# A further combined k-pair in seven paired products of a hybrid decoder layer

## The chip, the cores and the metric

The kernel runs on one core of a Trainium2 chip. The metric is the time of one execution on the device, in microseconds (us). The time before is the median of 3 runs, 1982.21 us (1981.88 to 1982.49). A profile of one further execution gives the times of single instructions. Engines are named as in the profile: PE is TensorE (matmuls), PEld its loading of the stationary operand, DVE is VectorE, ACT is ScalarE, POOL is GpSimd, SP is SyncE, which issues the DMAs.

## The reference

One decoder layer in float32 over 256 tokens of width 2048:

```python
hn = rmsnorm(h, norm_mix_w)
q, k, v, g_ret, xr, yr, g_a, g_b = jnp.split(hn @ w_in, offsets, axis=-1)
ret_out = silu(g_ret) * head_groupnorm(chunkwise_retention(q, k, v), ret_gn_w)
rnn_out = gelu(yr) * rg_lru(causal_dwconv(xr))
merged = sigmoid(g_a) * (ret_out @ w_proj_ret) + sigmoid(g_b) * (rnn_out @ w_proj_rnn)
h = h + merged @ w_mix_out
h = h + memory_cross_attention(rmsnorm(h, norm_xa_w), rmsnorm(mem), w_q, w_k, w_v, w_o)
gate, val = jnp.split(causal_dwconv(rmsnorm(h, norm_ffn_w) @ w_up), 2, axis=-1)
h = h + (silu(gate) * val) @ w_down
out = rmsnorm(h, final_norm_w)
```

Nearly all of the work is in the products with weights: `w_in` is 2048 x 14336, the projections are 2048 x 2048, `w_up` is 2048 x 11264 and `w_down` 5632 x 2048. The feed-forward width of 5632 is done in three parts of 4, 4 and 3 blocks of 512 columns.

## The kernel before

**Split operands.** Every operand of a product is held as two numbers of the type fp32r, `hi` (the value rounded) and `lo` (what the rounding left). A product of two tiles is then three matmuls: hi x hi, lo x hi, hi x lo (`products_n`, `rows_of`). For weights, ScalarE writes `hi` as a cast (L349) and VectorE writes `lo` as a difference (L350), for two slices of 128 rows at a time (128 x 1024). There are 6 buffers for `hi` and 6 for `lo` (`PART_BUFS`), and 3 for raw weights (`RAW_BUFS`), which SP loads in one order fixed on the host (`weight_stream`).

**Products.** `steps_n` computes 256 tokens x 512 columns. It walks over the inner dimension in chunks of four slices. `steps_pair` computes two such blocks of 512 columns at once and walks in k-pairs, two slices of 128 rows at a time: eight k-pairs for an inner dimension of 2048. A plain k-pair is 8 tile products, 24 matmuls. They go into four banks of PSUM: `p2` and `p4` for the first block of columns (two token halves), `x3` and `n` for the second.

**Combined k-pairs.** For the k-pairs listed in the tuple `seven`, the pair is treated as a 2 x 2 block product (token halves by slices, slices by column blocks) and computed with seven products in place of eight, by sums of blocks in the manner of Strassen and Winograd: 21 matmuls. This needs

- four sums of weight blocks on VectorE, in place in the raw buffer (L370 in `seven_parts`), and seven weight parts to split in place of four: three splits of 128 x 1024 and one of 128 x 512;
- sums of the token blocks, made once per operand and kept (`sums_of`, L448 to L459): one sum of hi and lo where the unsplit value is gone, three differences `tq`, a cast by ScalarE and a difference `ts`;
- four more banks of PSUM, `p1`, `p6`, `p7`, `x5`. After the last k-pair in the tuple, a copy by ScalarE (L513) and four operations of VectorE (L520) bring them together as `o`, and after the last k-pair of the product four more (L530) add `p2`, `p4`, `x3` and `n`.

The tuples are `SEVEN = (2, 5)` for most pairs, `SEVEN_O = (3, 5)` for the attention's output, `SEVEN_U = (4,)` for the up products, and `SEVEN_V = (5,)` for the second pair of values.

**Order of the work.** `weight_plan` lists the products: q, k, v and gates of the retention in two groups; eight products of the recurrent branch with their conversions between; the gate `g_b` and `w_proj_rnn`, alternating; two pairs for `g_a` (columns from O_GA, "first" and "second gate pair") and two for `w_proj_ret`; `w_mix_out`; attention; then the feed-forward parts. In these, one up pair (a gate block and its value block) precedes the down products of the part before, and the others follow: up 0 to 3, up 4, down of part one, up 5 to 7, up 8, down of part two, up 9 and 10, last down. A down product of the first two parts is two pairs, each with the four blocks' hidden activations `hid` (eight k-pairs) as its left operand.

Inside a product, `chunks` prefetches weights two chunks ahead and, after each chunk, runs what `later(n, ...)` has put off by n chunks: turning finished rows by DMA (`by_dma`, two copies to `pl` by ScalarE, a DMA transpose, two copies back as `f`, L565), splitting the heads of the retention (`split_head`, during the two `g_a` pairs), the convolutions of the up products (L1136, L1138) and their gates (`gate_up`, L1147 to L1150, with splits at L588 and L589). Matmuls keep the order in which they are written. On the other engines a scheduler of the compiler decides the order in the queue, with a priority for some steps; once built, every queue is fixed and works in order, so that a late instruction delays all that stand behind it.

Of the kernel before, what the change touches and what calls it, by code (L numbers as in the profile page):

```python
# [38 lines left out]
GN_EPS = 1e-5  # L39
FF_PARTS = [4, 4, 3]  # L40
EARLY = [2, 2, 4, 4, 4]
SEVEN = (2, 5)
SEVEN_O = (3, 5)
SEVEN_U = (4,)
SEVEN_V = (5,)

O_Q, O_K, O_V, O_G = 0, 1024, 2048, 4096
O_XR, O_YR, O_GA, O_GB = 6144, 8192, 10240, 12288
# [26 lines left out]
def weight_plan():  # L75

    plan = []
    for g in range(2):
        keys = [("w_in", 0, NT, c + g * BW) for c in (O_Q, O_K)]
        values = [("w_in", 0, NT, O_V + b * BW) for b in range(2)]  # L80
        plan += keys + [both("w_in", O_V + 1024, SEVEN_V)] if g else [keys[0], values[0], keys[1], values[1]]
        plan.append(both("w_in", O_G + g * 1024))
    for b in range(4):
        plan += [("w_in", 0, NT, c + b * BW) for c in (O_XR, O_YR)]
    plan += [("w_in", 0, NT, O_GB + b * BW) for b in range(2)] + [both("w_proj_rnn", 0)]
    plan += [both("w_in", O_GB + 1024), both("w_proj_rnn", 1024)]
    plan += [both(w, c + b * BW) for w, c in (("w_in", O_GA), ("w_proj_ret", 0)) for b in (0, 2)]
    plan += [("w_mix_out", 0, NT, b * BW) for b in range(4)]
    plan += [(w, 0, NT, b * BW) for b in range(4) for w in ("xa_w_k", "xa_w_q")]
    plan += [("xa_w_v", 0, NT, b * BW) for b in range(4)]  # L90
    plan += [both("xa_w_o", 0, SEVEN_O)] + [("xa_w_o", 0, NT, b * BW) for b in (2, 3)]
    for kind, *a in ff_plan():
        if kind == "down" and sum(a) < NF // 4:
            plan += [both("ffn_w_down", b * BW, SEVEN, a[0] * BW, 4 * a[1]) for b in (0, 2)]
        elif kind == "down":
            plan += [("ffn_w_down", a[0] * BW, 4 * a[1], b * BW) for b in range(4)]
        else:
            plan.append(both("ffn_w_up", a[0] * BW, SEVEN_U, apart=FF))
    return plan


# [64 lines left out]
def hybrid_layer(  # L166
# [305 lines left out]
            sums_of(t, src, scale)  # L472
        out.append(t)

    def steps_pair(w, row, st, nk, c1, c2, seven=SEVEN):

        last = max(seven)
        banks, begun = {}, set()
        banks["p2"], banks["p4"] = (lambda a: (a[:, 0, :], a[:, 1, :]))(acc())
        banks["x3"], banks["n"] = (small((P, BW)) for _ in range(2))  # L480

        def rows_of(name, left, right, end):

            o = banks[name]
            for i, (a, b) in enumerate(((0, 0), (1, 0), (0, 1))):
                mm(o, left[a], right[b], start=name not in begun, stop=end and i == 2, skip_group_check=True)
                begun.add(name)

        o1 = o2 = None
        for k0, n, parts in chunks(nk, w, row, (c1, c2, seven)):  # L490
            k2 = k0 // KH
            for i in seven:
                if k2 < i <= k2 + 3 and (not isinstance(st, list) or i < len(st)):
                    sums_of(st[i])
            t = st[k2]
            own = [
                [(t[:, j, i * P : (i + 1) * P], t[:, j, S + i * P : S + (i + 1) * P]) for j in range(2)]
                for i in range(2)
            ]
            if k2 in seven:  # L500
                if "p1" not in banks:
                    for a, b in (("p1", "p6"), ("p7", "x5")):
                        two = acc()
                        banks[a], banks[b] = two[:, 0, :], two[:, 1, :]
                ts = sums_of(t)
                s3, s1, s2, s4 = ((ts[:, 0, i, :], ts[:, 1, i, :]) for i in range(4))
                lefts = (own[0][0], s4, own[0][1], s1, s3, s2, own[1][1])
                for name, l, r in zip(("p1", "x3", "p2", "x5", "p7", "p6", "p4"), lefts, parts):
                    rows_of(name, l, r, k2 == last and name in ("p1", "x5", "p7", "p6"))
                if k2 == last:  # L510
                    o1, o2 = (big([P, 2, BW], s="o") for _ in range(2))
                    with tc.high_priority(FREE):
                        act.copy(o1[:, 0, :], banks["p1"])  # L513
                        for o, a, b, op in (
                            (o2[:, 0, :], o1[:, 0, :], banks["p6"], ALU.add),
                            (o1[:, 1, :], o2[:, 0, :], banks["p7"], ALU.add),
                            (o2[:, 1, :], banks["x5"], o1[:, 1, :], ALU.subtract),
                            (o2[:, 0, :], banks["x5"], o2[:, 0, :], ALU.subtract),
                        ):
                            dve.tensor_tensor(out=o, in0=a, in1=b, op=op)  # L520
            else:
                end = k0 + n == nk
                for b, names in enumerate((("p2", "p4"), ("x3", "n"))):
                    for tt, name in enumerate(names):
                        for j in range(KH):
                            rows_of(name, own[tt][j], parts[b * KH + j], end and j == KH - 1)
            yield o1, o2
        with tc.high_priority(FREE):
            for o, a in ((o1[:, 0, :], "p2"), (o1[:, 1, :], "p4"), (o2[:, 0, :], "x3"), (o2[:, 1, :], "n")):
                dve.tensor_tensor(out=o, in0=o, in1=banks[a], op=ALU.add)  # L530
# [212 lines left out]
    def split_head(h):  # L743
        f = words[h // 2][:, 2 * (h % 2) : 2 * (h % 2) + 2, :]
        ret.append(split_cols(f, lambda j: half_gn[:, 2 * h + j : 2 * h + j + 1]))
        if h in SEVEN:
            sums_of(ret[h])

    def retain(g, qr, kr, vs, dec, gates):
# [63 lines left out]
    for g in range(2):  # L813
        dec = big([P, 4, S], s="dec")
        vs, turned = [], ([], [])
        for b, o in enumerate((O_Q, O_K)):

            def rotate_both(f, o=turned[b]):
                o.append(rotated(f[:, 0:2, :]))
                later(0, lambda: o.append(rotated(f[:, 2:4, :])))  # L820

            a = gemm_n("w_in", 0, xs, NT, o + g * BW) if g + b else q0
            turned_rows(a, rs0, rotate_both, 2 - b if g + b else 3, g + b > 0)
            if b == 1:
                sp.dma_start(
                    out=dec,
                    in_=consts[:, C_DEC + g * 4 * S : C_DEC + (g + 1) * 4 * S].rearrange("p (h s) -> p h s", s=S),
                )
            if g == 0:
                v = gemm_n("w_in", 0, xs, NT, O_V + b * BW) if b else ended(v_steps)  # L830
                vs.append(split_rows(v, rs0))
        if g == 1:
            vs += [split_rows(v, rs0) for v in pair("w_in", 0, xs, NT, O_V + 1024, O_V + 1024 + BW, SEVEN_V)]
        qr, kr = turned
        gates = []
        c = O_G + g * 1024
        for a in pair("w_in", 0, xs, NT, c, c + BW):
            t = big([P, 2, BW], s="gate")
            for tt in range(2):
                act.activation(t[:, tt, :], a[:, tt, :], AF.Tanh, scale=half_rs0[:, tt : tt + 1])  # L840
            dve.scalar_tensor_tensor(out=a, in0=t, scalar=1.0, in1=a, op0=ALU.add, op1=ALU.mult)
            gates.append(a)
        retain(g, qr, kr, vs, dec, gates)
# [164 lines left out]
    def residual(w, st, out, wcol, steps=None):  # L1008
# [4 lines left out]
        for b in range(4):  # L1013
            if steps:
                steps(b)
                if b == 0:
                    for one in products[:3]:
                        for _ in range(2):
                            next(one)
            elif b == 0:  # L1020
                sources += pair(w, 0, st, NT, 0, BW, SEVEN_O)
            h = hrow[b]
            dve.tensor_add(h, h, sources.pop(0) if sources else ended(products[b]))
            by_dma(h, lambda f, b=b: turn(f, b, out, wcol), 1 + (b == 1), b == 3 and steps is None)
            if b < 2:
                later(2 + b, lambda h=h, b=b: squares(h, ss, b))
            else:
                squares(h, ss, b)
# [211 lines left out]
    def up(b, hid, seven):  # L1240
# [4 lines left out]
            conv(f, NF + 4 * b, vl)  # L1245
            gate_up(gt, vl, hid, seven)

        two = pair("ffn_w_up", 0, h2s, NT, b * BW, FF + b * BW, SEVEN_U)
        for a, then, wait in zip(two, (lambda f: conv(f, 4 * b, gt), value), (1, 3)):
            with tc.high_priority(FREE):  # L1250
                for tt in range(2):
# [4 lines left out]
    for kind, b, *n in ff_plan():  # L1256
        if kind == "up":
            b0 = max(one[1] for one in ff_plan() if one[0] == "down" and one[1] <= b)
            seven = tuple(i - 2 * (b - b0) for i in SEVEN) if b0 < sum(FF_PARTS[:2]) else ()
            up(b, hid.setdefault(b, []), seven)  # L1260
        else:
            final = b + n[0] == NF // 4
# [48 lines left out]
```

## Time and profile before

| what | value |
|---|---|
| median of 3 runs | 1982.21 us |
| profiled execution | 1980.76 us |
| its span, from the first to the last instruction | 1979.0 us |
| PE busy | 1965.8 us, 99% |
| DVE busy | 1564.5 us, 79% |
| ACT busy | 1367.1 us, 69% |
| granted TensorE clock, mean | 0.999 |

A row of a group of instructions reads: line, engine, operation, output<-inputs, shapes, x count | busy us, mean ns of one | idle time of the engine ahead of them, and what ended it. A row of the timeline reads: start, length, engine, line, operation, output<-inputs, x count of instructions merged, and in brackets the engine's idle time ahead of it with what ended it. A row of waits reads: engine, line <- what it waited for: us in total, times, longest. Successive instructions of an engine overlap a little, so that busy time is less than count times mean.

### The profile page before, as it was taken

To read this page: it belongs to the slowest core of one execution; us is meant where nothing else is said; L and a number is where in the kernel's file an instruction comes from. 1 tells how busy PE (TensorE), PEld (TensorE's weight loads), DVE (VectorE), ACT (ScalarE), POOL (GpSimd) and SP (SyncE) were. 2 spreads that over 40 slices of the span, in tenths; PEclk is the share of its full clock that TensorE was granted. 3 is DMA by queue.
4 is the path that set the end of the run, shared out by engine and by line. 5 is a ranking of instruction groups with operands and counts; after the bars stand their busy time and mean duration, and the time that the engine had idled before them with its cause. 6 is when DMAs were issued, how large, how long until landed. Compare 5 with 4: busy or idle time off the path is not lost.

```text
span 1979.0 us, 24013 instructions
## 1 busy us (share of the span) xinstructions
PE 1965.8 (99%) x8834; PEld 1631.4 (82%) x8834; DVE 1564.5 (79%) x2050; ACT 1367.1 (69%) x1671; POOL 26.8 (1%) x25
## 2 busy tenths in 40 slices
PE   9999999999999999999999999999999999999998
PEld 7888788888888888888888888888888888888887
DVE  6887986899898888767555567778889878898686
ACT  7666657989654656697676667777776578774683
POOL 0000010010000000000000000000000000000000
PEclk9999999999999999999999999999999999999999
DMA  9755567666555465887676657666666566666673
GB/s 334 238 213 173 194 232 203 213 210 212 194 212 189 176 228 192 297 277 226 218 222 206 203 170 223 210 216 213 224 207 208 212 211 215 215 210 233 214 252 110
DMA packets 197190, 425.62 MB, mean 215 GB/s; under 512 B 142032, under 2 KB 146640, under 8 KB 152016
## 3 DMA queue, kind: packets, MB, share of 16 engines
q1 hardware_dynamic: 197072, 424.09, 64.2%
q8 instruction: 69, 1.13, 0.2%
q14 instruction: 49, 0.40, 0.1%
HBM read 388.39 MB, written 2.10 MB: 197 GB/s over the span
## 4 chain that ended last, share of the span: by engine, by line
PE 91%; DVE 3%; ACT 3%; issue 1%; DMA 1%; SPq 0%; POOL 0%; POOLq 0%; DVEq 0%; ACTq 0%
PE acc L251 66%; PE sm L251 25%; DVE lo L350 1%; DMA raw<-in_wall 1%; ACT hi L349 1%; ACT f L565 1%; ACT pl L552 0%; DMA pt<-pl 0%; DVE xr L932 0%; DVE tb L734 0%; ACT rows L804 0%; DMA raw<-in_head 0%; DVE fv L1138 0%; DVE o L530 0%; DVE raw L370 0%
## 5 line engine op out<-in xcount | busy, mean ns | idle before, releaser
L251 PE MATMUL acc<-hi,s 128*128 128x512 f32 (+1 forms) x3976 | 1218.7, 388 | 0.2 <-ACT s L611 0.2
L350 DVE TENSOR_TENSOR lo<-raw,hi 128x1024 fp32r<-128x1024 f32 (+1 forms) x794 | 931.8, 1197 | 325.7 <-ACT hi L349 315.8
L349 ACT CAST hi<-raw 128x1024 fp32r<-128x1024 f32 (+1 forms) x794 | 788.3, 1023 | 401.1 <-PE acc L251 126.6
L251 PEld LDWEIGHTS acc<-hi,s 128*128 128x128 f32 x3976 | 743.4, 188 | 152.4 <-ACT s L611 0.5
L251 PE MATMUL acc<-lo,s 128*128 128x512 f32 (+1 forms) x1988 | 771.0, 388 | 1.4 <-DVE lo L350 1.4
L251 PEld LDWEIGHTS acc<-lo,s 128*128 128x128 f32 x1988 | 373.3, 188 | 79.8 <-DVE lo L350 3.1
L251 PE MATMUL sm<-hi,s 128*128 128x512 f32 x1344 | 414.0, 389 | 1.6 <-DVE o L530 1.6
L251 PEld LDWEIGHTS sm<-hi,s 128*128 128x128 f32 x1344 | 252.1, 188 | 55.0 <-ACT v L600 1.8
L251 PE MATMUL sm<-lo,s 128*128 128x512 f32 x672 | 261.5, 389 | 0.0
L565 ACT COPY f<-pt 128x1024 uint16<-128x1024 uint16 x128 | 167.1, 1353 | 36.2 <-DMA pt<-pl 35.8
L251 PEld LDWEIGHTS sm<-lo,s 128*128 128x128 f32 x672 | 126.2, 188 | 26.1
L370 DVE TENSOR_TENSOR raw<-raw 128x512 f32<-128x512 f32 x160 | 110.0, 687 | 2.4
L251 PE MATMUL acc<-hi,ts 128*128 128x512 f32 x240 | 73.9, 389 | 0.0
L552 ACT COPY pl<-rows 128x1024 uint16<-128x1024 uint16 x56 | 55.7, 1042 | 24.8 <-DVE rows L576 13.3
L552 ACT COPY pl<-o 128x1024 uint16<-128x1024 uint16 x52 | 51.6, 1038 | 6.7 <-DVE o L1000 6.7
L251 PEld LDWEIGHTS acc<-hi,ts 128*128 128x128 f32 x240 | 45.0, 188 | 9.3
L251 PE MATMUL acc<-lo,ts 128*128 128x512 f32 x120 | 47.1, 393 | 1.4 <-DVE lo L350 1.3
L1138 DVE SCALAR_TENSOR_TENSOR fv<-f,pf,fv 128x255 f32<-128x255 f32 (+1 forms) x88 | 38.3, 476 | 0.0
L530 DVE TENSOR_TENSOR o<-o,acc 128x512 f32<-128x512 f32 x52 | 33.2, 678 | 5.7 <-PE acc L251 5.7
L1138 DVE SCALAR_TENSOR_TENSOR fg<-f,pf,fg 128x255 f32<-128x255 f32 (+1 forms) x88 | 35.8, 477 | 0.0
L520 DVE TENSOR_TENSOR o<-o,acc 128x512 f32<-128x512 f32 x52 | 35.2, 678 | 0.0
L530 DVE TENSOR_TENSOR o<-o,sm 128x512 f32<-128x512 f32 x52 | 33.9, 677 | 0.1
(190 smaller groups left out, 1010.8 us busy)
## 6 DMA issues: line engine op xcount, KB each, us to landing
raw<-in_wall SPq DMA_DIRECT2D x352, 1024.0 KB, 4.9
nat<-in_x SPq DMA_DIRECT2D x8, 512.0 KB, 9.2
raw<-in_wall SPq DMA_DIRECT2D x7, 512.0 KB, 6.2
pt<-pl SPq DMA_TRANSPOSE x128, 3.3
nat<-in_mem SPq DMA_DIRECT2D x4, 512.0 KB, 8.9
xt<-in_x_t SPq DMA_DIRECT2D x3, 512.0 KB, 9.3
xt<-in_mem_t SPq DMA_DIRECT2D x3, 512.0 KB, 6.4
dec<-in_consts SPq DMA_DIRECT2D x2, 512.0 KB, 4.4
```

The source lines that it names most:

```text
L251: tc.keep_in_program_order(pe.matmul(*a, **k))
L349: act.copy(hi[:, cs], src[:, cs])
L350: dve.tensor_tensor(out=lo[:, cs], in0=src[:, cs], in1=hi[:, cs].bitcast(F32), op=ALU.subtract)
L370: dve.tensor_tensor(out=o, in0=a, in1=b, op=ALU.add)
L520: dve.tensor_tensor(out=o, in0=a, in1=b, op=op)
L530: dve.tensor_tensor(out=o, in0=o, in1=banks[a], op=ALU.add)
L552: act.copy(planes[:, tt], words[:, tt])
L565: act.copy(halves_[:, :, :, cs], turned_[:, :, :, cs])
L1138: dve.scalar_tensor_tensor(out=y[:, s:S], in0=z[:, j, 0 : S - s], scalar=pf[:, 2 - s, t : t + 1], in1=y[:, s:S], op0=ALU.mult, op1=ALU.add,)
```

## The change

- `SEVEN` becomes (2, 6) in place of (2, 5), and `SEVEN_V` becomes (6,) in place of (5,): in these pairs the last combined k-pair is k-pair 6.
- A new tuple `MORE = (2, 4, 6)` is used for the second gate pair, the second pair of `w_proj_ret`, and the second pair of both paired down products: three combined k-pairs in place of two.
- A new tuple `MORE_U = (2, 4)` is used for the up pair that follows something other than an up pair in the plan (blocks 0, 5 and 9): two in place of one.
- Token sums are made for heads 2, 4 and 6 of `ret` and for the matching tiles of `hid`, in place of 2 and 5.
- `steps_pair` reads its tuple from the plan, and is not given it any more.

Nothing else is edited. The host packs the weights of a combined k-pair in another order of slices, as before.

```diff
-SEVEN = (2, 5)
+SEVEN = (2, 6)
+MORE = (2, 4, 6)
 SEVEN_O = (3, 5)
 SEVEN_U = (4,)
-SEVEN_V = (5,)
+MORE_U = (2, 4)
+SEVEN_V = (6,)
...
-    plan += [both(w, c + b * BW) for w, c in (("w_in", O_GA), ("w_proj_ret", 0)) for b in (0, 2)]
+    for w, c in (("w_in", O_GA), ("w_proj_ret", 0)):
+        plan += [both(w, c), both(w, c + 1024, MORE)]
...
-            plan += [both("ffn_w_down", b * BW, SEVEN, a[0] * BW, 4 * a[1]) for b in (0, 2)]
+            plan += [both("ffn_w_down", b * BW, MORE if b else SEVEN, a[0] * BW, 4 * a[1]) for b in (0, 2)]
...
-            plan.append(both("ffn_w_up", a[0] * BW, SEVEN_U, apart=FF))
+            plan.append(both("ffn_w_up", a[0] * BW, MORE_U if plan[-1][0] != "ffn_w_up" else SEVEN_U, apart=FF))
...
-    def steps_pair(w, row, st, nk, c1, c2, seven=SEVEN):
+    def steps_pair(w, row, st, nk, c1, c2):
+        seven = plan[gemms[0]][3][2]
...
-        if h in SEVEN:
+        if h in MORE:
             sums_of(ret[h])
...
-            seven = tuple(i - 2 * (b - b0) for i in SEVEN) if b0 < sum(FF_PARTS[:2]) else ()
+            seven = tuple(i - 2 * (b - b0) for i in MORE) if b0 < sum(FF_PARTS[:2]) else ()
```

More of the change, by code (lines that the diff above doesn't have):

```diff
@@ L832, in hybrid_layer @@
         if g == 1:
-            vs += [split_rows(v, rs0) for v in pair("w_in", 0, xs, NT, O_V + 1024, O_V + 1024 + BW, SEVEN_V)]
+            vs += [split_rows(v, rs0) for v in pair("w_in", 0, xs, NT, O_V + 1024, O_V + 1024 + BW)]
         qr, kr = turned
@@ L1020, in residual @@
             elif b == 0:
-                sources += pair(w, 0, st, NT, 0, BW, SEVEN_O)
+                sources += pair(w, 0, st, NT, 0, BW)
             h = hrow[b]
@@ L1246, in value @@
             gate_up(gt, vl, hid, seven)
-        two = pair("ffn_w_up", 0, h2s, NT, b * BW, FF + b * BW, SEVEN_U)
+        two = pair("ffn_w_up", 0, h2s, NT, b * BW, FF + b * BW)
         for a, then, wait in zip(two, (lambda f: conv(f, 4 * b, gt), value), (1, 3)):
```

## The prediction

> **What bounds the kernel now.** I read the busy shares first, then the chain that ended last, then who waits for whom on TensorE, and last busy time by stage.
>
> ```profile
> span 1979.0 us, 24013 instructions
> PE 1965.8 (99%) x8834; PEld 1631.4 (82%) x8834; DVE 1564.5 (79%) x2050; ACT 1367.1 (69%) x1671; POOL 26.8 (1%) x25
> PE 91%; DVE 3%; ACT 3%; issue 1%; DMA 1%; SPq 0%; POOL 0%; POOLq 0%; DVEq 0%; ACTq 0%
> 1219.43 46.24 PE acc L251 x204
> ```
>
> TensorE is busy 99% and carries 91% of the chain. A stretch of 204 matmuls without a gap gives 46.24 / 204 = 0.2267 us each. So a matmul less is worth 0.227 us, as long as TensorE does not then wait.
>
> ```profile
> PE acc L251 <- DVE lo L350: 2.6, 5, 0.8
> PE sm L251 <- DVE o L530: 1.6, 2, 1.4
> 217.52 0.50 PE L251 MATMUL acc<-lo,ts 128*128 128x512 f32 x1 [0.48 <-DVE lo L350]
> 233.76 0.70 PE L251 MATMUL sm<-hi,s 128*128 128x512 f32 x2 [1.44 <-DVE o L530]
> 235.60 0.73 PE L251 MATMUL sm<-hi,s 128*128 128x512 f32 x2 [0.20 <-DVE o L530]
> ...
> 1459.36 0.50 PE L251 MATMUL acc<-lo,ts 128*128 128x512 f32 x1 [0.79 <-DVE lo L350]
> 1510.99 0.50 PE L251 MATMUL acc<-lo,s 128*128 128x512 f32 x1 [0.85 <-DVE lo L350]
> 1767.26 0.50 PE L251 MATMUL acc<-lo,s 128*128 128x512 f32 x1 [0.28 <-DVE lo L350]
> ```
>
> TensorE's few waits all name VectorE: twice it adds up a finished product too late (L530), else it has not split the next weights (`lo`, L350). They lie in the second value pair (217 to 236 us) and around the two middle feed-forward down products. There VectorE already has no cover.
>
> ```profile
> 676.20:718.40 42.20, 42.20 (x188) 34.96 (x187) 40.85 (x57) 27.79 (x37) 0.00 (x0) 1.00 0.58 220
> 760.60:802.80 42.20, 42.20 (x188) 34.96 (x187) 37.03 (x44) 29.30 (x33) 0.00 (x0) 1.00 0.60 199
> 1478.40:1521.50 43.10, 42.25 (x187) 34.66 (x186) 40.17 (x59) 36.41 (x45) 0.00 (x0) 1.00 0.68 212
> 1521.50:1563.70 42.20, 42.20 (x188) 34.95 (x187) 38.91 (x43) 20.70 (x22) 0.00 (x0) 1.00 0.62 235
> ```
>
> Busy time by stage (columns: length, PE, weight loads, DVE, ACT, POOL, clock, DMA share, GB/s): second gate pair, second retention projection, first down product and its second half. VectorE is busy 97%, 88%, 93% and 92% of these, not 79%. Three of the four take a further combination, the first down product a shifted one.
>
> **The change part by part.** *Matmuls.* A combined k-pair takes 21 matmuls in place of 24. Seven products get one more: 21 matmuls, 21 x 0.2267 = **-4.8 us**, all on the path.
>
> *VectorE's price of a combination.*
>
> ```profile
> L350 DVE TENSOR_TENSOR lo<-raw,hi 128x1024 fp32r<-128x1024 f32 x748 | 902.0, 1229 | 323.1 <-ACT hi L349 313.2 <-PE acc L251 4.0
> L370 DVE TENSOR_TENSOR raw<-raw 128x512 f32<-128x512 f32 x160 | 110.0, 687 | 2.4
> L350 DVE TENSOR_TENSOR lo<-raw,hi 128x512 fp32r<-128x512 f32 x46 | 31.1, 684 | 2.6 <-ACT hi L349 2.6
> L448 DVE TENSOR_TENSOR g<-s 128x512 f32<-128x512 f32 x9 | 6.1, 682 | 0.0
> L459 DVE TENSOR_TENSOR ts<-tq,ts 128x512 fp32r<-128x512 f32 x11 | 7.5, 684 | 0.7 <-ACT ts L458 0.7
> L454 DVE TENSOR_TENSOR tq<-g 128x256 f32<-128x256 f32 x9 | 3.8, 419 | 0.1
> L455 DVE TENSOR_TENSOR tq<-tq,g 128x128 f32<-128x128 f32 x9 | 2.6, 287 | 0.2
> L456 DVE TENSOR_TENSOR tq<-g,tq 128x128 f32<-128x128 f32 x9 | 2.5, 283 | 0.0
> 1533.38 7.04 DVE L350 TENSOR_TENSOR lo<-raw,hi 128x1024 fp32r<-128x1024 f32 x6
> ```
>
> A plain k-pair costs two splits, 2 x 1.229 = 2.46 us. A combined one costs three of these, a half one and four sums of weights: 3 x 1.229 + 0.684 + 4 x 0.687 = 7.12. That is 4.66 more, against TensorE's 4.76 us for the same k-pair. Six splits in a row take 7.04, so each following instruction overlaps by about 0.06; I use 1.17, 0.62 and so on below. A new token sum costs 0.68 + 0.42 + 0.29 + 0.28 + 0.68 = 2.36 (1.66 where the source is already there). Five are new: one each of `xs`, `ret` and `h2s`, two of `hid`. Together 7 x 4.66 + 3 x 2.36 + 2 x 1.66 = 43 us, less 65 instructions x 0.06 = 39: VectorE goes from 1564.5 to about 1604, 81% over all. ScalarE gains 19 instructions, some 13 us.
>
> [...]
>
> *Second gate pair.* In the changed program's order VectorE ends the former pair's four sums, and until the last split of combined k-pair 6 it has: 14 splits of 1.17, 3 of 0.62, 12 weight sums of 0.63, four token sums (two before) of 4 x (0.62 + 1.42), and ten `ret` splits of 0.42:
>
> ```profile
> 678.88 1.46 DVE L530 TENSOR_TENSOR o<-o,sm 128x512 f32<-128x512 f32 x2
> ...
> 679.45 0.61 PE L251 MATMUL acc<-hi,s 128*128 128x512 f32 x2
> ...
> L612 DVE SCALAR_TENSOR_TENSOR s<-f,pb,s 128x256 fp32r<-128x256 f32 x48 | 20.6, 478 | 0.0
> ```
>
> 16.4 + 1.9 + 7.5 + 8.2 + 4.2 = 38.2 us. The sums now end 0.9 us into the product (680.34, its first matmul at 679.45); the new order puts a few more steps ahead of them, so I take 1.4. The split is then there at 39.6. TensorE needs it after k-pairs 0 to 5 (four of 24 and two of 21 matmuls, 31.3 us) and 17 of k-pair 6's matmuls (3.85): at 35.1. **+4.5 us** (2 to 6: less if some `ret` splits hide in gaps, more if VectorE waits for ScalarE inside the four token sums).
>
> *Second retention projection.* Its k-pair 4 becomes a combination just where ScalarE is late with `merged`:
>
> ```profile
> 780.34 2.54 ACT L565 COPY f<-pt 128x1024 uint16<-128x1024 uint16 x2
> 783.82 1.23 DVE L350 TENSOR_TENSOR lo<-raw,hi 128x1024 fp32r<-128x1024 f32 x1 [1.98 <-ACT hi L349]
> 788.02 0.39 PE L251 MATMUL sm<-lo,s 128*128 128x512 f32 x1
> ```
>
> The k-pair's second split ends at 785.05 and is used at 788.02: 3.0 us of cover. The new order puts two splits of `merged`, a weight sum and the third split there (ending 787.2, needed at 787.35), then a sum, its copy by ScalarE and the last split (790.1, needed at 788.7): **+1.5 us** (0 to 3.5).
>
> *Down products.* In each first down product the second combination moves from k-pair 5 to 6, and the order puts all value convolutions and gates ahead of it.
>
> ```profile
> 1497.28 4.09 DVE L350 TENSOR_TENSOR lo<-raw,hi 128x1024 fp32r<-128x1024 f32 x4
> 1502.50 0.39 PE L251 MATMUL sm<-lo,s 128*128 128x512 f32 x1
> 1507.54 1.66 DVE L1138 SCALAR_TENSOR_TENSOR fv<-f,pf,fv 128x255 f32<-128x255 f32 x4
> L1148 DVE SCALAR_TENSOR_TENSOR fo<-ft,fg 128x512 f32<-128x512 f32 x22 | 14.9, 683 | 0.0
> 1530.61 2.85 DVE L370 TENSOR_TENSOR raw<-raw 128x512 f32<-128x512 f32 x4
> ...
> 1541.72 1.82 DVE L350 TENSOR_TENSOR lo<-raw,hi 128x1024 fp32r<-128x1024 f32 x2 [1.29 <-ACT hi L349]
> ...
> 1554.96 1.22 DVE L350 TENSOR_TENSOR lo<-raw,hi 128x1024 fp32r<-128x1024 f32 x1 [1.67 <-ACT hi L349]
> ```
>
> K-pair 4's splits (the first two of the four in the first row) end at 1499.6. Then come two splits (2.34), eight convolutions of 0.42 and five gate steps of 0.62 (6.4), and of the combination split, step, half split, four dependent sums, split (1.17 + 0.62 + 0.62 + 2.85 + 1.17): 15.2, so 1514.8. TensorE starts k-pair 5 ten matmuls after 1502.50, at 1504.8, and needs the result 24 + 11 matmuls later, at 1512.7: late by 2.1, where 0.85 was waited. That is 1.25 more; up to 2.7 more if the third `hid` sum of each part (1.4 us, ahead of it) shifts the whole chain, as ScalarE's copies start from these sums. I take 2.2 each, nearer the upper end as VectorE waits nowhere long here (40.17 of 43.10): **+4.4 us** for two parts (2.5 to 5.4; 0 if the order hides it). The second halves get their added combination at k-pair 4, where VectorE now idles 1.29 and 1.67 us around it; its 4.4 us (4.66 less overlap) eat this and 1.4 us of cover from the k-pairs after: 0 (to 1).
>
> *Value pair.* Its one combination moves from 5 to 6, past the rotations, and the four sums of its end now stand ahead of the value splits: of 0.48 + 1.44 + 0.20 = 2.1 us most goes: **-1.7 us** (-2.1 to 0).
>
> *First up pairs and the rest.*
>
> ```profile
> 1273.93 1.23 DVE L350 TENSOR_TENSOR lo<-raw,hi 128x1024 fp32r<-128x1024 f32 x1 [1.88 <-ACT hi L349]
> ...
> 1285.00 0.39 PE L251 MATMUL acc<-lo,s 128*128 128x512 f32 x1
> ```
>
> The first up pair's split for k-pair 4 is ready at 1275.2 and used at 1285.0, 9.8 us ahead. A combination and `h2s[2]`'s sum before it (4.4 + 2.1) leave about 3. The other pairs whose second combination moves to 6 only bunch eight end sums ahead of the next pair's first combination. Small waits: **+0.5** (0 to 2). DMA bytes are unchanged; SP's weight loads keep their order, and three raw buffers are released later only where VectorE is late already.
>
> Sum: -4.8 - 1.7 + 4.5 + 1.5 + 4.4 + 0.5 = **+4.4 us** on 1980.76 (span 1979.0 and 1.76 around it), 1985.2. The runs' median, 1982.21, lies 1.45 above the profiled execution, so **1986.6 us**.
>
> **The rivals.** *Cover holds* (the other side): the matmuls go and VectorE's queues stay ahead, since its non-urgent work (`ret` splits, convolutions) drains elsewhere. For it: TensorE waits nowhere in three of the four stages shown; against it: VectorE is busy 97% of the second gate pair already, and a combination there costs it as much time as TensorE has for the k-pair. It decides where the new waits stay under 6.5 us in sum (under 2.5 for a gain beyond 0.2%). At no lateness at all 1982.2 - 4.8 - 1.7 = 1975.7. [...] *A draw*: the shift of 1.4 us is swallowed in the down products (2.5 in place of 4.4) and the retention projection's wait fails to show: 1986.6 - 1.9 - 1.5 = 1983.2. For it: VectorE has 2.9 us without work in the first down product; against it: TensorE waits there all the same. *ScalarE too*: ScalarE, busy 36.41 of 43.10 there, falls behind in turn and the upper ends come together, 6 + 3.5 + 5.4 + 2 with 0 from the value pair: 1982.2 - 4.8 + 16.9 = 1994.3. For it: VectorE's longest wait is for ScalarE's `hi`; against it: ScalarE gains only 13 us over all. That the matmuls do not go is excluded: the changed program has 8806 in place of 8827.
>
> **How the numbers follow.** Forecast 0.48, draw 0.25, cover holds 0.14, ScalarE too 0.13. Of the forecast 0.39 lies beyond 0.2% (4 us, about what a measurement here can tell from no change) and 0.09 within; the draw lies within; so slower 0.39 + 0.13 = 0.52, same 0.34, faster 0.14. The range leaves out most of the cover's case and the last end of ScalarE's: 1979.5 to 1993.5; the forecast's own is 1983 to 1990.
>
> **What would show it.** Busy TensorE falls by 4.8 to about 1961, VectorE rises by 39 to about 1604. Waits of TensorE for `lo` grow from 2.6 to about 12 us, in the second gate pair (k-pairs 4 to 6), near 790, 1512 and 1768; the wait of 1.44 for L530 goes. Wrong if the second gate pair shows no wait (then VectorE's order had more cover than my count), or if waits name DMA or ScalarE.

## The result, and the profile after

The changed kernel takes 1998.98 us (median of 6 runs, 1996.83 to 2000.45), the kernel before 1981.95 us in the same comparison (6 runs, 1979.89 to 1982.49): a ratio of 1.0086, 95% interval 1.0073 to 1.0099. It is slower by 17 us. The forecast was 1986.6 us with a range up to 1993.5: right in its sign, far too small in its size, and the time lies outside the range. The profiled execution of after took 1996.83 us, the fastest of its six; its span is 16.0 us longer than before's.

The page of after, its busy shares, and the four longest of TensorE's rows of waits:

```profile
span 1995.0 us, 24071 instructions
PE 1968.0 (99%) x8813; PEld 1628.8 (82%) x8813; DVE 1602.2 (80%) x2115; ACT 1378.7 (69%) x1690; POOL 31.7 (2%) x25
PE acc L254 <- ACT hi L352: 8.5, 5, 5.5
PE acc L254 <- DVE lo L353: 4.0, 7, 0.7
PE sm L254 <- DVE ts L462: 2.2, 2, 1.1
PE sm L254 <- DVE o L534: 1.7, 1, 1.7
```

(Lines are 3 or 4 further down than before: L254 is the matmul of L251, L352 and L353 the cast and the split of L349 and L350, L534 the closing sums of L530.) The largest wait is a new one, 8.5 us for ScalarE's `hi`, 5.5 of them at one place. The main single waits on TensorE's timeline:

```profile
233.94 0.73 PE L254 MATMUL sm<-hi,s 128*128 128x512 f32 x2 [1.69 <-DVE o L534]
...
566.72 0.50 PE L254 MATMUL sm<-hi,ts 128*128 128x512 f32 x1 [1.08 <-DVE ts L462]
...
704.41 0.51 PE L254 MATMUL sm<-hi,ts 128*128 128x512 f32 x1 [0.95 <-ACT ts L461]
706.01 0.50 PE L254 MATMUL sm<-hi,ts 128*128 128x512 f32 x1 [1.09 <-DVE ts L462]
...
794.58 0.50 PE L254 MATMUL acc<-lo,ts 128*128 128x512 f32 x1 [0.64 <-DVE lo L353]
...
847.11 1.22 PE L254 MATMUL acc<-hi,s 128*128 128x512 f32 x2 [5.49 <-ACT hi L352]
...
1527.74 0.73 PE L254 MATMUL acc<-hi,ts 128*128 128x512 f32 x2 [1.46 <-ACT hi L352]
...
1785.48 0.73 PE L254 MATMUL acc<-hi,ts 128*128 128x512 f32 x2 [0.51 <-ACT hi L352]
```

For a ledger I took, from each trace, the time between the starts of successive matmuls less the 0.2267 us of a matmul, wherever that is over 0.15 us; for most waits it is about 0.16 us more than the bracket shows (5.65 for the 5.49 at 847.11), and it also counts what matmuls at a lower clock lose.

| place | before, us | after, us | difference |
|---|---|---|---|
| second value pair, 215 to 236 | 2.9 | 2.6 | -0.3 |
| second `g_b` pair, 566 | 0 | 1.7 | +1.7 |
| second gate pair, 704 to 722 | 0 | 4.5 | +4.5 |
| second retention projection, 795 to 798 | 0 | 2.2 | +2.2 |
| `w_mix_out`, 839 before and 847 after | 0.4 | 7.6 | +7.2 |
| down products of part one | 2.0 | 4.1 | +2.1 |
| down products of part two | 0.4 | 1.6 | +1.1 |
| 21 matmuls fewer | | | -4.8 |

Before rounding these give 13.8 of the 16.0 us; of the rest, 1.6 us are smaller steps, 0.9 of them between 700 and 800 us, and 0.6 us the tail after the last matmul. Of the ledger's losses about 3.5 us are matmuls at a lower clock: 1.98 behind the wait at `w_mix_out` and 1.56 in the down products of part one (last section).

The 7.2 us at `w_mix_out` come out of SP's queue. SP's rows there, first of before, then of after (`raw` is a weight load, `nat` a load of the residual's or the memory's rows, `pt` a transpose), each followed by ScalarE's first cast of a weight (`hi`) after them:

```profile
814.84 0.52 SPq L222 DMA_DIRECT2D raw<-in_wall  x1
815.46 4.94 SPq L553 DMA_TRANSPOSE pt<-pl  x2
820.45 2.11 SPq L218 DMA_DIRECT2D nat<-in_x  x4
822.66 2.17 SPq L222 DMA_DIRECT2D nat<-in_mem  x4
824.93 25.69 SPq L222 DMA_DIRECT2D raw<-in_wall  x7
...
837.07 2.00 ACT L349 CAST hi<-raw 128x1024 fp32r<-128x1024 f32 x2 [6.50 <-DMA raw<-in_wall]
```

```profile
822.85 3.99 SPq L557 DMA_TRANSPOSE pt<-pl  x3
826.94 0.53 SPq L221 DMA_DIRECT2D nat<-in_x  x1
...
828.79 1.73 SPq L221 DMA_DIRECT2D nat<-in_x  x3
830.62 2.56 SPq L225 DMA_DIRECT2D nat<-in_mem  x4
833.27 24.70 SPq L225 DMA_DIRECT2D raw<-in_wall  x7
...
846.02 1.99 ACT L352 CAST hi<-raw 128x1024 fp32r<-128x1024 f32 x2 [11.14 <-DMA raw<-in_wall]
```

Before, one weight load goes out at 814.84, ahead of two transposes and of the eight row loads. In after that load (in both traces the 153rd of weights) stands behind them: it is issued at 833.27, ScalarE gets it at 846.02 and waits 11.14 us for it, where it had waited 6.50 before for the load of 824.93. This is what TensorE's 5.49 us are, under the name of ScalarE. The chain of waits of each kernel, before and then after, has the same step, the load and the time until it has landed:

```profile
824.93 12.04 DMA raw<-in_wall
```

```profile
833.27 12.64 DMA raw<-in_wall
```

These two loads, each the first behind the row loads, landed 12.04 and 12.64 us after their issue, and the slowest of the seven in either row 13.8 us after it, where the median weight load of after takes 4.8 us (the page's DMA issues; the last column is the time from issue to landing):

```profile
raw<-in_wall SPq DMA_DIRECT2D x352, 1024.0 KB, 4.8
```

Before, another load had still gone out in time, and 12 us were nearly covered; in after none had.

### The profile page after: what moved, and what is told of

Same layout as the page of the kernel before. It is cut to its first block, busy times and chain, and to the rows that moved or that the text cites. A ratio compares the mean times of both kernels' runs of the same rounds, so it can differ in the third digit from the quotient of the medians.

```text
span 1995.0 us, 24071 instructions
## 1 busy us (share of the span) xinstructions
PE 1968.0 (99%) x8813; PEld 1628.8 (82%) x8813; DVE 1602.2 (80%) x2115; ACT 1378.7 (69%) x1690; POOL 31.7 (2%) x25
## 4 chain that ended last, share of the span: by engine, by line
PE 88%; DVE 5%; ACT 4%; issue 2%; DMA 1%; SPq 0%; POOL 0%; POOLq 0%; DVEq 0%; ACTq 0%
PE acc L254 65%; PE sm L254 23%; DVE lo L353 2%; ACT hi L352 2%; ACT f L569 1%; DMA raw<-in_wall 1%; DVE raw L373 1%; ACT pl L556 0%; DVE fv L1142 0%; DVE o L524 0%; DVE xr L936 0%; DVE o L534 0%; DMA raw<-in_head 0%; DVE s L593 0%; ACT o L1256 0%
## 5 line engine op out<-in xcount | busy, mean ns | idle before, releaser
L254 PE MATMUL acc<-hi,s 128*128 128x512 f32 x3962 | 1216.9, 389 | 5.7 <-ACT hi L352 5.5
L353 DVE TENSOR_TENSOR lo<-raw,hi 128x1024 fp32r<-128x1024 f32 (+1 forms) x808 | 944.8, 1198 | 307.7 <-ACT hi L352 302.3
L352 ACT CAST hi<-raw 128x1024 fp32r<-128x1024 f32 (+1 forms) x808 | 796.5, 1020 | 411.4 <-DVE raw L373 125.2
L254 PEld LDWEIGHTS acc<-hi,s 128*128 128x128 f32 x3962 | 741.9, 188 | 158.9 <-ACT hi L352 6.2
L254 PE MATMUL acc<-lo,s 128*128 128x512 f32 x1981 | 768.9, 388 | 0.5 <-DVE lo L353 0.4
L254 PEld LDWEIGHTS acc<-lo,s 128*128 128x128 f32 x1981 | 372.4, 188 | 78.4 <-DVE lo L353 2.0
L254 PE MATMUL sm<-hi,s 128*128 128x512 f32 x1288 | 396.7, 389 | 1.7 <-DVE o L534 1.7
L254 PEld LDWEIGHTS sm<-hi,s 128*128 128x128 f32 x1288 | 241.7, 188 | 52.3 <-DVE o L534 2.1
L254 PE MATMUL sm<-lo,s 128*128 128x512 f32 x644 | 250.5, 389 | 0.0
L254 PEld LDWEIGHTS sm<-lo,s 128*128 128x128 f32 x644 | 120.9, 188 | 25.0
L373 DVE TENSOR_TENSOR raw<-raw 128x512 f32<-128x512 f32 x188 | 129.9, 691 | 3.0
L254 PE MATMUL acc<-hi,ts 128*128 128x512 f32 x282 | 87.8, 393 | 3.0 <-ACT hi L352 3.0
L254 PEld LDWEIGHTS acc<-hi,ts 128*128 128x128 f32 x282 | 52.9, 189 | 15.4 <-ACT hi L352 4.8
L254 PE MATMUL acc<-lo,ts 128*128 128x512 f32 x141 | 56.2, 398 | 3.6 <-DVE lo L353 3.6
L254 PEld LDWEIGHTS acc<-lo,ts 128*128 128x128 f32 x141 | 26.6, 189 | 12.0 <-DVE lo L353 6.7
L524 DVE TENSOR_TENSOR o<-o,acc 128x512 f32<-128x512 f32 x52 | 35.7, 687 | 0.3
L534 DVE TENSOR_TENSOR o<-o,acc 128x512 f32<-128x512 f32 x52 | 34.3, 689 | 1.9 <-PE acc L254 1.9
```

Of the source, the lines that this page charges most:

```text
L254: tc.keep_in_program_order(pe.matmul(*a, **k))
L352: act.copy(hi[:, cs], src[:, cs])
L353: dve.tensor_tensor(out=lo[:, cs], in0=src[:, cs], in1=hi[:, cs].bitcast(F32), op=ALU.subtract)
L373: dve.tensor_tensor(out=o, in0=a, in1=b, op=ALU.add)
```

## The experiments

Every ratio is against the kernel before, run beside it on the same chip (1982.74 us for the first four, 1982.65 us for the last four).

**The row loads, later.** In the changed kernel the eight row loads are issued in the middle of the products of `w_mix_out`:

```diff
-    hrow = [load_rows(x, c) for c in range(4)]
-    mnat = [load_half(mem, i) for i in range(4)]
+    hrow, mnat = [], []
+    def load_residual():
+        hrow.extend(load_rows(x, c) for c in range(4))
+        mnat.extend(load_half(mem, i) for i in range(4))
...
-                    for one in products[:3]:
-                        for _ in range(2):
+                    for i, one in enumerate(products[:3]):
+                        for j in range(2):
                             next(one)
+                            if (i, j) == (2, 0):
+                                load_residual()
```

> The changed kernel, but the eight row loads (x and mem, 512 KB each) are issued two weight loads later on SP's queue, behind the weights that the first mix_out chunks need. Theory A (one weight load had come to stand behind the eight row loads, and the TensorE gap of 5.5 us then also lowered the granted clock for some 4 us): the wait near 842 us and the slow matmuls after it go, 7.4 us in all, so about 1991.5 us; all other waits stay. Rival B (the 4 MB of the row loads, or VectorE's late sums of the second retention projection, hold mix_out up whatever stands in front): the wait stays above 4 us, 1996 us or more.

Measured: 1991.26 us, ratio 1.0035 (1.0020 to 1.0049), 7.7 us less than after. SP now has two weight loads ahead of the row loads:

```profile
828.03 0.52 SPq L225 DMA_DIRECT2D raw<-in_wall  x1
...
829.94 0.57 SPq L225 DMA_DIRECT2D raw<-in_wall  x1
830.55 2.99 SPq L221 DMA_DIRECT2D nat<-in_x  x4
```

TensorE waits nowhere between 838 and 852 us, though the earlier waits, in the gate pair and the retention projection, stand as they were. So the order in SP's queue, and not VectorE's lateness alone, makes this wait. That the medians differ by as much as the ledger says, 7.7 and 7.6 us, is in part chance: this trace has two new waits of together 1.3 us at 904 and 915 us, and in its down products no matmul at a lower clock.

**Second retention projection undone.**

```diff
-        plan += [both(w, c), both(w, c + 1024, MORE)]
+        plan += [both(w, c), both(w, c + 1024, MORE if w == "w_in" else SEVEN)]
...
-        if h in MORE:
+        if h in SEVEN:
             sums_of(ret[h])
```

> The changed kernel with k-pairs (2, 6) in place of (2, 4, 6) in the second retention projection (and no token sum of head 4). Theory A: this further combination is what moved the weight load behind the row loads; without it the mix_out wait (7.4 us with the slow clock) and the waits near 795 us (2.2 us) go and three matmuls come back (+0.7): about 1990 us. Rival B (the order of the queue has another cause, as the shifted combinations): the mix_out wait stays, about 1997 us.

Measured: 1987.77 us, ratio 1.0025 (1.0016 to 1.0034): one of the seven further k-pairs, with its token sum, accounts for 11 us. SP's rows and what is left of TensorE's waits in the gate pair and at `w_mix_out`:

```profile
820.11 0.53 SPq L225 DMA_DIRECT2D raw<-in_wall  x1
820.68 5.26 SPq L557 DMA_TRANSPOSE pt<-pl  x2
825.99 2.12 SPq L221 DMA_DIRECT2D nat<-in_x  x4
```

```profile
707.70 0.50 PE L254 MATMUL acc<-lo,ts 128*128 128x512 f32 x1 [0.55 <-DVE lo L353]
717.75 0.50 PE L254 MATMUL acc<-lo,ts 128*128 128x512 f32 x1 [0.70 <-DVE lo L353]
...
844.68 0.73 PE L254 MATMUL acc<-hi,s 128*128 128x512 f32 x2 [1.93 <-ACT hi L352]
```

The weight load is ahead of the row loads again, so it is this combination, or the token sum that went with it, that moved it, and the wait at `w_mix_out` falls from 7.6 to 2.8 us. The 2.2 us in the projection are gone. And the gate pair loses 1.6 us where it lost 4.5, although its own combinations are untouched: what went there is the token sum of head 4.

**The shift alone.** The kernel before with `SEVEN = (2, 6)` and `SEVEN_V = (6,)`, nothing else:

> The kernel before with only the positions changed: (2, 6) in place of (2, 5), values (6,) in place of (5,); as many matmuls as before. Theory A (the later combination bunches eight end sums ahead of the next pair's token sums and weights): new waits of 1.7 us near 565 us, 0.4 in the value pair and about 1.2 in each first down product, 4.5 us slower, 1986.5 us. Rival B (positions cost nothing, all waits come from the further combinations): 1982 us within 1, and no wait near 565.

Measured: 1989.14 us, ratio 1.0029 (1.0019 to 1.0040). The shift, which removes no matmul, costs 6.4 us. Its trace has the waits of after at the places that only the shift touches:

```profile
566.39 0.50 PE L251 MATMUL sm<-hi,ts 128*128 128x512 f32 x1 [1.09 <-DVE ts L459]
...
1515.47 0.73 PE L251 MATMUL acc<-hi,ts 128*128 128x512 f32 x2 [1.19 <-ACT hi L349]
...
1776.58 0.73 PE L251 MATMUL acc<-hi,ts 128*128 128x512 f32 x2 [1.27 <-ACT hi L349]
```

By the ledger: `g_b` pair 1.7, `w_mix_out` 1.6 (0.4 before), down products 3.8 and 3.0 (2.0 and 0.4 before), 1.6 of the 3.8 again at a lower clock. There are only two `hid` sums here, and the down products lose no less than with three. The 1.6 at `w_mix_out` need not come from the shift: the kernel of the next experiment is not changed up to there, has SP's rows in before's order, and loses 1.85 at the same place.

**The first up pairs alone.** The kernel before with the further combination in these three only:

```diff
+MORE_U = (2, 4)
...
-            plan.append(both("ffn_w_up", a[0] * BW, SEVEN_U, apart=FF))
+            plan.append(both("ffn_w_up", a[0] * BW, MORE_U if plan[-1][0] != "ffn_w_up" else SEVEN_U, apart=FF))
```

> The kernel before with only the further combination in the up pairs of blocks 0, 5 and 9: nine matmuls fewer. Theory A (VectorE has some 10 us of cover there): 9 x 0.2267 = 2.0 us faster, 1980.0 us, with no new wait. Rival B (any further combination costs VectorE as much as it saves TensorE): 1982 us or more, with waits for lo near 1285 us.

Measured: 1980.53 us, ratio 0.9987 (0.9978 to 0.9997), a small gain. No wait appears in the up products of the first part; here, where VectorE has 9.8 us of cover, the matmuls are a net gain. In the later parts one wait is new, 0.4 us at 1718.

**Second gate pair undone.**

```diff
-        plan += [both(w, c), both(w, c + 1024, MORE)]
+        plan += [both(w, c), both(w, c + 1024, SEVEN if w == "w_in" else MORE)]
```

> The changed kernel with the second gate pair back to (2, 6), one part undone; the token sum of head 4 stays, for the second retention projection. Theory A (each wait belongs to its place and cause): the second gate pair's 4.5 us of waits go nearly all (its combined k-pair 4 costs VectorE 4.66 us at 97% load; without the sum of head 4 the same waits had already shrunk to 1.6), 21 matmuls come back (+1 x 0.2267 x 3 = 0.68 us), and the wait at w_mix_out (5.6 us and the slow clock behind it) stays, since one weight load still stands behind the row loads: about 1999 - 4.5 + 0.7 = 1995. Theory B (VectorE is behind over the whole stretch, and what it does not wait for here it waits for later): the waits move into the retention projections, and the time stays at about 1999.

Measured: 1995.55 us, ratio 1.0060 (1.0046 to 1.0074). Busy time in the gate pair's stretch, after first and then this kernel (columns as in the prediction):

```profile
676.20:723.00 46.80, 43.25 (x186) 34.32 (x185) 45.46 (x72) 28.36 (x42) 0.00 (x0) 1.00 0.42 151
```

```profile
676.20:722.00 45.80, 45.80 (x203) 37.92 (x202) 44.46 (x67) 29.77 (x43) 0.00 (x0) 1.00 0.55 201
```

With the token sum of head 4 but without the combination, VectorE is just as full (97%) and TensorE has no idle time at all. The sum alone costs nothing, the combination alone 1.6 us (the second experiment), both together 4.5: this stage, with VectorE at 97%, pays for what goes over the edge. The wait at `w_mix_out` stays and even grows, from 5.49 to 6.37 us in its row and from 7.6 to 9.5 us in the ledger, of which about half is the clock. So the two places are not wholly apart: the wait in the gate pair goes for good, but some of what it cost comes back later. The time falls by 3.4 us where the theory of separate causes had 4; the theory of one general lag would have kept 1999. (Three matmuls come back, not 21 as the expectation has it; its 0.68 us are those of three.)

**One pair before the `g_b` pair shifted back.** The kernel with the later row loads, and the first pair of `w_proj_rnn` at (2, 5) again:

```diff
-[both("w_proj_rnn", 0)]
+[both("w_proj_rnn", 0, (2, 5))]
```

> The kernel rows_late (1991.3 us) with one more edit: the first pair of w_proj_rnn alone goes back to (2, 5). Theory A (the 1.7 us that TensorE waits near 566 for the token sum of the second g_b pair come from the eight closing sums of the pair before, which the shift to k-pair 6 bunches into one run of VectorE): that wait goes, though the token sum and the second g_b pair itself are untouched: 1991.3 - 1.7 = 1989.6. Theory B (the token sum is late of itself, or the second g_b pair's own shift makes it late): the wait stays at 1.7 us and the time at 1991.3.

Measured: 1990.02 us, ratio 1.0035 (1.0021 to 1.0049). The gain expected, 1.7 us, is smaller than what the times can tell apart, but the trace decides: TensorE waits nowhere between 560 and 570 us. VectorE's rows ahead of the place, of the kernel with only the row loads moved and of this one:

```profile
552.50 0.68 DVE L534 TENSOR_TENSOR o<-o,acc 128x512 f32<-128x512 f32 x1
553.10 1.28 DVE L524 TENSOR_TENSOR o<-acc,o 128x512 f32<-128x512 f32 x2
...
554.89 1.27 DVE L534 TENSOR_TENSOR o<-o,sm 128x512 f32<-128x512 f32 x2
...
560.70 0.68 DVE L451 TENSOR_TENSOR g<-s 128x512 f32<-128x512 f32 x1
...
567.25 0.68 DVE L462 TENSOR_TENSOR ts<-tq,ts 128x512 fp32r<-128x512 f32 x1
```

```profile
547.09 0.68 DVE L524 TENSOR_TENSOR o<-o,acc 128x512 f32<-128x512 f32 x1
...
549.42 0.68 DVE L451 TENSOR_TENSOR g<-s 128x512 f32<-128x512 f32 x1
...
564.97 0.68 DVE L462 TENSOR_TENSOR ts<-tq,ts 128x512 fp32r<-128x512 f32 x1
```

With the combination at k-pair 5, its four sums (L524) are spread among splits, and the token sum of the next pair starts at 549.42. At k-pair 6 they fall together with the pair's four closing sums (L534), and the token sum starts at 560.70, 11 us later; its last step (L462) starts 2.3 us later. The token sum itself and the pair that uses it are the same in both.

**Two versions meant to be faster.** The kernel of the first up pairs with the row loads later (the edit of the first experiment):

> The kernel up_only (the kernel before with a further combined k-pair in the first up pair of each part, 1980.5 us) with the eight row loads issued two chunks into the third product of w_mix_out, as in rows_late. Theory A (the row loads that stand in SP's queue with weight loads behind them are what TensorE waits for near 840, also before): the 1.15 + 0.7 us there go: 1980.5 - 1.85 = 1978.7. Theory B (the wait before was VectorE's own, as the waits row named it): 1980.5.

Measured: 1979.30 us, ratio 0.9980 (0.9971 to 0.9989). Two weight loads are ahead of the row loads here too, and TensorE does not wait between 835 and 846 us; the kernel of the up pairs alone had waited there:

```profile
840.31 0.73 PE L252 MATMUL acc<-hi,s 128*128 128x512 f32 x2 [1.00 <-ACT hi L350]
```

So the small wait that before's trace puts down to `lo` at 839 was most likely the row loads' as well. Then the down products: one combination in the first pair, three in the second, as many matmuls as before.

```diff
+DOWN = (4,), (2, 4, 6)
...
-            plan += [both("ffn_w_down", b * BW, SEVEN, a[0] * BW, 4 * a[1]) for b in (0, 2)]
+            plan += [both("ffn_w_down", b * BW, DOWN[b // 2], a[0] * BW, 4 * a[1]) for b in (0, 2)]
...
-            seven = tuple(i - 2 * (b - b0) for i in SEVEN) if b0 < sum(FF_PARTS[:2]) else ()
+            seven = tuple(i - 2 * (b - b0) for i in (2, 4, 6)) if b0 < sum(FF_PARTS[:2]) else ()
```

> up_rows, and in the two paired down products the first pair has one combined k-pair, (4,), and the second three, (2, 4, 6): as many matmuls as up_rows, with hid sums 2, 4, 6. Theory A (TensorE waits in the first down pair because VectorE has convolutions, gates, sums and two combinations there, and has room in the second): taking one combination from the first pair removes its waits, about 1.9 us in part one and 0.4 in part two, though a third token sum of 1.4 us is added: 1978.7 - 2.3 = 1976.4. Theory B (what makes the wait is the time of the combination that comes after the convolutions, not how many there are; or the third combination in the second half has no cover): 1978.7 or more.

Measured: 1978.30 us, ratio 0.9976 (0.9968 to 0.9985), the fastest of all. Of the expected 2.3 us 1.0 shows: by the ledger the down products lost 2.3 us in the former version and lose 1.1 here. Between 1455 and 1560 us are left only

```profile
1458.35 0.50 PE L253 MATMUL acc<-lo,ts 128*128 128x512 f32 x1 [0.27 <-DVE lo L352]
1502.16 0.50 PE L253 MATMUL acc<-lo,ts 128*128 128x512 f32 x1 [0.48 <-DVE lo L352]
```

and none in part two; the second pairs carry three combinations without a wait. This kernel beats the one before by 4 us. The intervals of the two versions overlap, so that the last step rests on the trace more than on the times.

## Why the prediction was right or wrong

*Matmuls, and VectorE's price.* Right: 21 fewer records, and VectorE at 1602.2 us where 1604 was worked out. ScalarE's 13 us came out as 11.6. Busy TensorE was to fall to about 1961 and rose to 1968.0: half of these 7 us are the 3.5 us that matmuls lost at a lower clock, and the rest is probably the 0.16 us around each wait and the small steps. TensorE's waits for `lo` were to grow from 2.6 to about 12 us and grew to 4.0; the others name ScalarE's `hi` and the token sums. One reading was short: before, two small waits (0.3 and 0.2 us) name ScalarE and not VectorE.

*Second gate pair, +4.5.* Right in its size, 4.5, and in its cause, a VectorE that is full; only in part in its place. The prediction has all of it at the last split of k-pair 6. There (718 to 722 us) 2.0 were lost, and 2.5 already in k-pair 4 (704 to 706 us), where TensorE waited for the token sum. It was the share by stage that told of it, and not the one over the whole span: VectorE is busy 80% of after's span, and 97% of this stage.

*Second retention projection, +1.5.* Measured 2.2, in k-pair 4 as forecast and inside the range; but its larger effect lay elsewhere (below).

*Down products, +4.4.* Measured +3.23, inside the range (2.5 to 5.4) by luck. The place was right, k-pair 6 behind the convolutions (1527.74), but 1.56 us of it are a lower clock, which I had not counted; without it the waits grew by 1.67, less than the range has. I took the upper end because of the third `hid` sum. The shift alone, with two sums, makes as much wait, so the third sum costs little or nothing.

*Value pair, -1.7.* Wrong: -0.3. The step that failed is that the four closing sums standing ahead of the value splits would end the wait of 1.44 us for L530. In after the combination at k-pair 6 puts its own four sums into the same run of VectorE, from 228.48 to 234.49, so the closing sums end no sooner, and the wait is 1.69.

*First up pairs and the rest, +0.5.* This is where the prediction broke. The up pairs were right (no wait). But the sentence "The other pairs whose second combination moves to 6 only bunch eight end sums ahead of the next pair's first combination" named a mechanism and priced it at nearly nothing; it costs 1.7 us before the `g_b` pair, as the run with one pair put back shows, and a like bunch kept the value pair's wait. And "SP's weight loads keep their order" was false: one weight load moved behind eight row loads, at 7.2 us (5.2 of waiting and 2.0 of lower clock). "Three raw buffers are released later only where VectorE is late already" missed that a later release is not only a later load, since loads of another kind may be put ahead: on SP's queue the eight row loads went out from 826.94 to 833.18 us and this weight load at 833.27, and it landed 12.64 us after its issue, where the median is 4.8. Without these two the sum of the other terms is -4.8 - 0.3 + 4.5 + 2.2 + 3.2 = +4.8. That it is so close to the forecast +4.4 is partly luck: the value pair and the retention projection came out 1.4 and 0.7 us dearer than forecast, the down products and the rest 1.2 and 0.5 us cheaper.

*Rivals.* None was this one. "ScalarE too" gave 1994.3 and the waits do name ScalarE's `hi` (8.5 us), but ScalarE is idle 11.14 us ahead of that cast: it waited for the DMA. The prediction's own test, "if waits name DMA or ScalarE", applied.

*What stays open.* Why the scheduler lets the load fall behind: the further combination in the retention projection or the token sum of head 4 causes it, by the run that undoes both, but which of the two, and by which buffer or priority, was not tried. The 2.2 us of after's loss in small steps and the tail were not attributed. That the bunch of sums makes the value pair's wait too is read from the trace; no run took it away there.

## What to carry to other kernels

When a change makes an engine later, compare the order of every DMA queue before and after, around each place where another kind of load waits its turn: one load that changed sides cost 7.2 us here, more than any of the computations (4.5 at most). Put the bulk loads that are not urgent behind the next weights (7.7 us less in the first experiment). Spend extra work by stage, where the engine that pays for it has cover (9.8 us in the first up pair, where no wait came), and spread sums that close one piece of work away from those of the next (1.7 us of waiting ahead of the `g_b` pair); a shift by one k-pair, which saves and adds nothing, cost 6.4 us.

## What the runs showed of the hardware

In after the granted clock fell at two places where TensorE waited, and that cost more time: 2.0 us behind a wait of 5.5, and 1.6 behind two waits that lost 2.5 together. Busy time in stretches of after (the seventh column is the clock), around the wait at `w_mix_out` and around the two waits in the first down product, and then the same place of the down product in the kernel with later row loads:

```profile
847.00:851.10 4.10, 3.95 (x9) 2.70 (x10) 3.88 (x4) 3.15 (x5) 0.00 (x0) 0.54 0.59 202
851.10:855.00 3.90, 3.90 (x19) 3.21 (x18) 3.20 (x3) 2.68 (x3) 0.00 (x0) 1.00 0.94 391
...
1526.00:1529.50 3.50, 1.32 (x5) 0.59 (x4) 3.40 (x5) 2.46 (x3) 0.00 (x0) 1.00 0.00 0
1529.50:1533.70 4.20, 4.20 (x13) 3.26 (x12) 4.20 (x5) 3.92 (x5) 0.00 (x0) 0.59 0.50 164
```

```profile
1522.00:1525.90 3.90, 1.60 (x6) 0.74 (x5) 3.77 (x6) 2.41 (x3) 0.00 (x0) 1.00 0.00 0
1525.90:1530.00 4.10, 4.10 (x19) 3.37 (x19) 4.10 (x5) 3.96 (x5) 0.00 (x0) 1.00 0.54 160
```

After 5.5 us without work the next 4.10 us are at 0.54: 9 matmuls in 4.10 us, then 19 in 3.90. In the down product two waits, which lose 1.6 and 0.9 us, are enough for 4.2 us at 0.59, about 1.6 us lost; in the other kernel waits of nearly the same size (TensorE is idle 2.30 us of 3.90 there, 2.18 of 3.50 in after) leave the clock at 1.00. The longer of after's two waits there is 1.46 us in its row.

How much idle time it took can be estimated from the traces of before and after, which record when the granted clock changes. Between 20 and 1960 us before's stays at 1.00; after's is at 0.5 for 6.83 us from 843.95 and for 3.41 us from 1530.03, and the 679.25 and 457.39 us from the end of each of these to the next change are, like the two stretches, whole multiples of 3.413 us (199 and 134 of them). I divided after's trace by this grid and took each matmul as 0.2267 us from its start. The two parts at full clock in which TensorE was idle longest, 2.49 us from 840.54 and 2.24 us from 1526.62, are the two that a stretch at 0.5 follows. None follows a part with less, at most 1.91 us (from 704.00). So for this one trace my estimate is a limit between 1.91 and 2.24 us of idle time in one part of the grid, in one piece or in several: the two waits of the down product lie in one part. Why waits of nearly the same size left the clock at 1.00 in the kernel with later row loads, this does not show.
